# Behind the mixers of a two-layer hybrid decoder: gates and projections with the tokens stationary, two retention heads as one block group

## The chip, the cores and the metric

The kernel runs on one core of one Trainium2 chip. The metric is the device time of one execution in microseconds (us), as the median of several runs. Of the core's engines this text uses TensorE (PE for its matmuls, PEld for its weight loads), VectorE (DVE), ScalarE (ACT), GpSimd (POOL) and SyncE (SP). The last two, and ACT, also issue DMA transfers; SP's and ACT's go through hardware queues, POOL's through a software queue.

## The reference

Two layers on an input x of 512 tokens by 1024 channels, float32. This is what the change touches of a layer:

```python
z = jnp.einsum('bsd,dc->bsc', x, w_in) + b_in
q_a, k_a, v_a, q_r, k_r, v_r, g_r, gate_a, gate_b = jnp.split(z, SPLIT_POINTS, axis=-1)
...
y_a = jnp.sum(wts[..., None] * jnp.stack(outs, axis=0), axis=0)     # attention, 384 wide
y_r = _retention(...)                                               # 4 heads of 512
y_b = (jax.nn.silu(g_r) * y_r.reshape(B, S, RET_V_WIDTH)).astype(x.dtype)
merged = (jax.nn.sigmoid(gate_a) * jnp.einsum('bsc,cd->bsd', y_a, w_attn_proj)
          + jax.nn.sigmoid(gate_b) * jnp.einsum('bsc,cd->bsd', y_b, w_ret_proj))
return jnp.einsum('bsd,de->bse', merged, w_out)
...
x = _layer_norm(ALPHA * x + mix, ln1_g[l], ln1_b[l])
```

Two mixers run side by side, dilated window attention (`y_a`) and retention with four heads (`y_b`). Each is projected to 1024 channels, each projection is multiplied by the sigmoid of 1024 columns of the input projection (`gate_a`, `gate_b`), and the sum goes through `w_out`. Then come the residual, a layer norm and a dense SwiGLU block of 2816 hidden features.

## The kernel before

**Numbers in two parts.** TensorE works on float32 rounded to its `fp32r` form. Every operand is therefore split into a high part, which ACT copies, and a low part, which DVE subtracts (`hilo`, L94 to L96), and a product is three matmuls: high with high, high with low, low with high. A weight arrives by `load` in one of eight buffers `raw` of 128x1024, and `unit` makes its two parts `whi` and `wlo`, in four buffers each.

**Block groups.** A large matrix product is cut into 2x2 blocks and done with seven block products in place of eight (Strassen's scheme in Winograd's form). On the left stand A11, A12, A22 and the four sums S1 to S4 of x, held in `xh`, `xl` and `xs`; on the right B11, B12, B21, B22 and sums of them that are made from the weights. A block product adds into one of a few PSUM banks, and what remains are a few additions of 512 columns. `wide` (L426) runs such a group with the weights stationary and 256 tokens moving, `tall` (L397) with 128 tokens stationary and up to 512 weight columns moving. `biased` (L482) is `tall` with a bias row: a matmul of one row of `pick` with `bh` puts the bias into PSUM first.

**Order of the work.** The program is written in the order of TensorE's work. Smaller pieces of it (turns, normalisations, loads) stand in a list `side`; after each three matmuls `tick` takes from it at a given rate (`rate`, `pace`, `drain`). Each engine runs its instructions in its own order, and a DMA that waits holds the DMAs behind it in the same engine's order. The buffers' release sets when SP can issue a load: a `raw` buffer is free when DVE has made the low part of the weight in it.

**The stages around the change**, in each layer:

1. The sigmoid columns (`gates`, L1087). Four pieces of 256 columns of `gate_a` paired with the same of `gate_b`, by `wide`. A result has the features on the partitions, so the bias goes into ACT's sigmoid, on 128x256. The sigmoids of `gate_a` stay in `sg`; those of `gate_b` go to `g_d` in DRAM (ACT's queue).
2. The attention projection (L1126 to L1143). `w_attn_proj` is stationary, the tokens move: 8 tiles of 9 matmuls of 512. DVE multiplies each tile with its `sg`, and POOL writes the product to `g_d`. Retention's output y is read back from `y_d` around this time: its first half is split into `xs`, the rest into `xh` and `xl`, whose x is no longer needed.
3. The retention projection (L1191 to L1215). For each of four pieces of 256 channels: four units of `w_ret_proj` as stationary weights, 2 x 16 x 3 matmuls of 512 tokens; then two gated additions of 128x512, and `hilo` into `m`, which has the features on the partitions, as the next stage wants it. No block group here: 384 matmuls.
4. `w_out` (L1229, `xstat`): `m` stationary, 512 columns moving, first columns 0 to 511 for all four token tiles, then the other half tile by tile; then residual, layer norm and the turn into `xh` and `xl` for the SwiGLU block.

Of the kernel before, what the change touches and what calls it, by code (L numbers as in the profile page):

```python
# [55 lines left out]
def hybrid_kernel(ctx, tc, x, rel_bias, w_in, b_in, w_attn_proj, w_ret_proj, w_out,  # L56
# [15 lines left out]
    NR = DEPTH * (RH + 2)  # L72
# [385 lines left out]

    def bias_rows():
# [4 lines left out]
        for q in (0, BK):  # L464
            for ly in range(DEPTH):
                for b2 in range(2):
                    o, e = b2 * RV, (C_VR, C_GR)[b2]
                    pool.dma_start(r[q + ly * RH:q + (ly + 1) * RH, o:o + RV],
                                   b_in[ly, e:e + RH * RV].rearrange("(h n) -> h n", h=RH))
                    e = C_VA + 2 * b2 * VB  # L470
                    pool.dma_start(r[q + va_row(ly, 0):q + va_row(ly, 2), o:o + VB],
                                   b_in[ly, e:e + 2 * VB].rearrange("(h n) -> h n", h=2))

# [34 lines left out]
    g_d = drp.tile([2, KD * P, S], F32, name="g_d")  # L508
# [169 lines left out]
    def layer(ly, cp):  # L678
# [4 lines left out]
        def bcol(c):  # L683
            return bT[:, c // P:c // P + 1]
# [304 lines left out]
        with stage("ret") as rp:  # L989
# [79 lines left out]
            ylow = xs.rearrange("p s h k t -> p (s h k t)").rearrange("p (h k t) -> p h k t", h=2, k=KD)  # L1069
            yraw = {}  # L1070

            def y_load(q):
                yraw[q] = load(y_v[:, 2 * q:2 * q + 2], 2, S)

            def y_parts(k):
                return (ylow[:, 0, k], ylow[:, 1, k]) if k < KD else (xh[:, k - KD], xl[:, k - KD])

            def y_put(q):
                if q < 4:
                    hilo(yraw[q], ylow[:, 0, 2 * q:2 * q + 2], ylow[:, 1, 2 * q:2 * q + 2])  # L1080
                else:
                    ks = slice(2 * q - KD, 2 * q - KD + 2)
                    hilo(yraw[q], xh[:, ks], xl[:, ks])

            def gates(dp, sa, sb):

                sn = {}  # L1087

                def put(o_, v, c, ts_):
# [3 lines left out]
                def ev(i, ps):  # L1093
                    p2 = ps.rearrange("p (q t) -> p q t", q=2)
                    if i in (1, 5, 6):
                        sn[i] = work("sn").rearrange("p (q t) -> p q t", q=2)
                        act.copy(out=sn[i], in_=p2)
                    elif i == 2:
                        dve.tensor_tensor(out=sn[1], in0=p2, in1=sn[1], op=ALU.add)
                        put(sa, sn[1], C_GA, slice(0, 256))  # L1100
                    elif i == 3:
                        dve.tensor_tensor(out=sn[6], in0=p2, in1=sn[6], op=ALU.subtract)
                        put(sb, sn[6], C_GB, slice(0, 256))
                    elif i == 7:
                        dve.tensor_tensor(out=sn[5], in0=sn[5], in1=p2, op=ALU.subtract)
                        put(sb, sn[5], C_GB, slice(256, 512))
                    elif i == 4:
                        put(sa, p2, C_GA, slice(256, 512))

                wide(pair_right(w_l[:, :, C_GA:], w_l[:, :, C_GB:], dp * 256), x_left, ev)  # L1110
                act.dma_start(g_d[1, dp * 256:(dp + 1) * 256].rearrange("(e p) s -> p e s", p=P), sb)

            pace(40)
            sgs, ya = [], []
# [5 lines left out]
            for dp in range(KD // 2):  # L1120
                if dp == KD // 2 - 1:
                    drain()
                    side.extend([nothing] * 4 + [lambda t=t: ya_put(t) for t in range(NG)] + [lambda q=q: y_load(q) for q in range(2)])
                    pace(18)
                sgs.append(slot("sg", F32))
                gates(dp, sgs[dp], rp.tile([P, 2, S], F32, tag="sb", name="sb"))  # L1126
            drain()
            was = [unit(load(wa_l[:, :, :256], NG, 256))]
            for dp in range(KD // 2):
                h, l = was[dp]  # L1130
                y_put(dp)
                if dp < 2:
                    y_load(dp + 2)
                if dp + 1 < KD // 2:
                    was.append(unit(load(wa_l[:, :, (dp + 1) * 256:(dp + 2) * 256], NG, 256)))
                for e in range(2):
                    cs = slice(e * P, (e + 1) * P)
# [4 lines left out]
                    dve.tensor_tensor(out=v, in0=v, in1=ps, op=ALU.mult)  # L1142
                pool.dma_start(g_d[0, dp * 256:(dp + 1) * 256].rearrange("(e p) s -> p e s", p=P), sgs[dp])  # L1143
# [4 lines left out]
        xt = fp.tile([P, NI, D], F32, name="xtok")  # L1148
# [8 lines left out]
        def norm(i, dst=None):  # L1157
            xi = xt[:, i]
# [12 lines left out]
        def residual(i, hf, ps, first, last):  # L1171
            o_ = xt[:, i, hf * 512:(hf + 1) * 512]
# [7 lines left out]
        with stage("mp") as mp:  # L1180

            m = mp.tile([P, 2, KD, S], F32R, name="m")
            xc = [[mp.tile([P, 4, 256], F32, name=f"xc{a}{b}") for b in range(2)] for a in range(2)]
            res = x if ly == 0 else spill
            pool.dma_start(xt, res.rearrange("(i p) d -> p i d", p=P))
            ln_par(mp.tile([P, 2 * D], F32, name="lnp"), ln1_g[ly], ln1_b[ly])

            def wr_unit(dp, h):
                return unit(load(wr_l[:, 4 * h:4 * h + 4, dp * 256:(dp + 1) * 256], 4, 256))

            for dp in range(KD // 2):  # L1191
                us = [wr_unit(dp, h) for h in range(2)]
                if dp == 0:
                    for q in range(4, 8):
                        y_load(q)
                    for q in range(4, 8):
                        y_put(q)
                us += [wr_unit(dp, h) for h in range(2, RH)]
                va, vb = (load(rows(g_d[b, dp * 256:(dp + 1) * 256]), 2, S) for b in range(2))
                pss = [psum("ps") for _ in range(2)]  # L1200
                for hh, (h, l) in enumerate(us):
                    for e in range(2):
                        cs = slice(e * P, (e + 1) * P)
                        for t in range(4):
                            k = 4 * hh + t
                            yh, yl = y_parts(k)
                            mm3(pss[e], h[:, t, cs], l[:, t, cs], yh, yl, k == 0, k == 4 * RH - 1)
                            tick(STEP)
                for e in range(2):
                    d = 2 * dp + e  # L1210
                    sa, sb = va[:, e], vb[:, e]
                    dve.tensor_tensor(out=sb, in0=sb, in1=pss[e], op=ALU.mult)
# [231 lines left out]
```

## Time and profile before

| | |
|---|---|
| median of 3 runs | 2108.03 us (2107.03 to 2109.09) |
| the profiled execution | 2107.58 us, span 2105.4 us, mean granted TensorE clock 0.999 |
| PE busy | 2089.3 us, 99% of the span |
| DVE, ACT, POOL busy | 1585.6 us (75%), 1114.0 us (53%), 260.5 us (12%) |
| moved by DMA | 363.91 MB, a mean of 173 GB/s |
| one execution of the four stages in layer 0 | gates within 476 to 565.65 us, attention projection to 582.0, retention projection to 669, then `w_out` |

The profile lists the busy time of each engine, the chain of work that ended last, groups of instructions by line (count, busy time, mean duration of one, idle time in front of them and what ended it), the DMA issues, and a timeline. A matmul's listed duration is its whole passage through the pipelined array; what it costs is the distance to the next one, which the chain gives: a stretch of the chain divided by its matmuls. Within a gates stage of the first layer, 30 matmuls and 16 turns of the retention stage before it are mixed in.

### The profile page before, as it was taken

How to read it: one execution, taken by the hardware profiler on the slowest of the kernel's cores; microseconds unless marked ns; L12 is line 12 of the kernel's file. 1: busy time of each engine (PE TensorE's matmuls, PEld its weight loads, DVE VectorE, ACT ScalarE, POOL GpSimd, SP SyncE). 2: the span in 40 equal slices, each digit the busy share in tenths (PEclk: the TensorE clock that was granted, in tenths of full speed). 3: DMA queues.
4: the chain of work that ended last, by engine and by line, in shares of the span. 5: the costliest groups of instructions: out<-in, count | busy, mean ns of one | idle time of the engine just before them, and what ended most of it. 6: DMA issues, size and time to landing. Idle time of an engine off the chain costs nothing.

```text
span 2105.4 us, 34894 instructions
## 1 busy us (share of the span) xinstructions
PE 2089.3 (99%) x13818; PEld 1898.4 (90%) x13818; DVE 1585.6 (75%) x2281; ACT 1114.0 (53%) x1723; POOL 260.5 (12%) x265
## 2 busy tenths in 40 slices
PE   9999999999999999999999999999999999999998
PEld 8989888889988898999899898888899889989897
DVE  7666888787644798887787578887867357988876
ACT  5567655556623364555355765555666233655551
POOL 4111111111000101111030111111000001110101
PEclk9999999999999999999999999999999999999999
DMA  8966467677776168868258555758677761687771
GB/s 245 218 169 146 125 156 180 178 187 175 228 265 200 44 155 206 193 164 216 85 158 224 146 129 132 193 142 209 164 195 242 237 200 36 174 196 177 194 195 42
DMA packets 319940, 363.91 MB, mean 173 GB/s; under 512 B 22429, under 2 KB 251969, under 8 KB 319648
## 3 DMA queue, kind: packets, MB, share of 16 engines
q1 hardware_dynamic: 229888, 257.20, 39.5%
q0 software_dynamic: 62608, 91.68, 23.2%
q10 hardware_dynamic: 27280, 12.80, 2.1%
q8 instruction: 108, 1.77, 0.3%
q14 instruction: 56, 0.46, 0.1%
HBM read 335.84 MB, written 28.53 MB: 173 GB/s over the span
## 4 chain that ended last, share of the span: by engine, by line
PE 92%; issue 4%; DVE 1%; DMA 1%; ACT 1%; POOL 0%; SPq 0%; POOLq 0%; DVEq 0%; ACTq 0%
PE ps L84 83%; PE px L84 6%; DMA raw<-in_w_in 1%; PE px L576 1%; PE px L1035 1%; PE px L193 0%; DVE wlo L351 0%; POOL ry L135 0%; ACT whi L345 0%; PE px L642 0%; DVE xtok L1167 0%; DMA raw<-in_w_ffn_gate 0%; ACT s L566 0%; DVE raw L363 0%; DVE raw L367 0%
## 5 line engine op out<-in xcount | busy, mean ns | idle before, releaser
L345 ACT CAST whi<-raw 128x1024 fp32r<-128x1024 f32 (+1 forms) x518 | 519.9, 1008 | 466.1 <-PE ps L84 198.8
L351 DVE TENSOR_TENSOR wlo<-raw,whi 128x1024 fp32r<-128x1024 f32 (+1 forms) x518 | 604.5, 1171 | 206.9 <-ACT whi L345 193.5
L84 PE MATMUL ps<-xs,whi 128*128 128x256 f32 (+1 forms) x2944 | 571.9, 293 | 0.4 <-ACT sn L807 0.4
L84 PEld LDWEIGHTS ps<-xs,whi 128*128 128x128 f32 x2944 | 467.5, 191 | 15.0 <-issue 1.7
L84 PE MATMUL ps<-xs,wlo 128*128 128x256 f32 (+1 forms) x1472 | 430.2, 292 | 0.6 <-DVE wlo L351 0.6
L84 PE MATMUL ps<-xh,whi 128*128 128x256 f32 (+1 forms) x1424 | 422.6, 298 | 2.7 <-ACT xh L95 2.2
L84 PE MATMUL ps<-xl,whi 128*128 128x256 f32 (+1 forms) x1424 | 419.5, 295 | 0.0
L84 PE MATMUL ps<-xh,wlo 128*128 128x256 f32 (+1 forms) x1424 | 418.7, 295 | 0.0
L84 PEld LDWEIGHTS ps<-xs,wlo 128*128 128x128 f32 x1472 | 281.6, 191 | 6.1 <-DVE wlo L351 1.1
L84 PEld LDWEIGHTS ps<-xh,whi 128*128 128x128 f32 x1424 | 271.0, 191 | 15.8 <-ACT xh L95 3.5
L84 PEld LDWEIGHTS ps<-xl,whi 128*128 128x128 f32 x1424 | 272.2, 191 | 8.3 <-DVE xl L96 0.6
L84 PEld LDWEIGHTS ps<-xh,wlo 128*128 128x128 f32 x1424 | 271.8, 191 | 6.5
L84 PE MATMUL ps<-whi,xs 128*128 128x512 f32 (+1 forms) x768 | 225.0, 362 | 0.8 <-ACT sn L490 0.8
L336 POOL DMA_DIRECT2D raw<-in_w_in x80 | 98.8, 1257 | 690.6 <-DVE wlo L351 271.8
L96 DVE TENSOR_TENSOR wlo<-raw,whi 128x1024 fp32r<-128x1024 f32 (+2 forms) x78 | 88.8, 1140 | 124.6 <-ACT whi L95 124.3
L367 DVE TENSOR_TENSOR raw<-raw 128x1024 f32<-128x1024 f32 (+1 forms) x148 | 173.8, 1174 | 8.0 <-DMA raw<-in_w_in 5.8
L84 PE MATMUL ps<-whi,ht 128*128 128x512 f32 x544 | 170.1, 391 | 0.0
L84 PEld LDWEIGHTS ps<-whi,xs 128*128 128x128 f32 x768 | 137.7, 188 | 20.3 <-ACT sn L490 1.0
L95 ACT CAST whi<-raw 128x1024 fp32r<-128x1024 f32 (+2 forms) x78 | 76.5, 982 | 140.1 <-PE ps L84 92.1
L84 PE MATMUL ps<-wlo,xs 128*128 128x512 f32 (+1 forms) x384 | 138.2, 360 | 0.3 <-DVE wlo L351 0.3
L84 PEld LDWEIGHTS ps<-whi,ht 128*128 128x128 f32 x544 | 101.8, 188 | 22.3 <-DVE ht L96 1.5
L336 POOL DMA_DIRECT2D raw<-in_w_ffn_gate x40 | 51.7, 1292 | 522.3 <-DMA raw<-in_w_ffn_up 222.6
(222 smaller groups left out, 2974.5 us busy)
## 6 DMA issues: line engine op xcount, KB each, us to landing
raw<-in_w_in SPq DMA_DIRECT2D x168, 512.0 KB, 5.0
raw<-in_w_in POOLq DMA_DIRECT2D x64, 512.0 KB, 8.1
raw<-in_w_ffn_up SPq DMA_DIRECT2D x64, 512.0 KB, 4.6
raw<-in_w_ffn_down SPq DMA_DIRECT2D x52, 512.0 KB, 4.7
raw<-in_w_ffn_gate SPq DMA_DIRECT2D x44, 512.0 KB, 4.9
raw<-in_w_ffn_gate POOLq DMA_DIRECT2D x40, 512.0 KB, 7.2
raw<-in_w_ret_proj SPq DMA_DIRECT2D x32, 512.0 KB, 6.7
raw<-in_w_in SPq DMA_DIRECT2D x56, 256.0 KB, 4.8
```

Of the source, the lines that this page charges most:

```text
L84: pe.matmul(ps, lhsT=a, rhs=b, start=start, stop=stop, skip_group_check=True)
L95: act.copy(out=hi, in_=src)
L96: dve.tensor_tensor(out=lo, in0=src, in1=hi.bitcast(F32), op=ALU.subtract)
L336: pool.dma_start(r, self.src({"P1": "B12", "P3": "B22"}[n], u), accum_op=ALU.add)
L345: act.copy(out=h, in_=src)
L351: dve.tensor_tensor(out=l, in0=src, in1=h.bitcast(F32), op=ALU.subtract)
L367: dve.tensor_tensor(out=r, in0=r, in1=self.t["B22" if n == "P2" else "B21", u], op=ALU.add)
L576: pe.transpose(px[:, hh, j * P:(j + 1) * P], ss[od][:, hh, j * P:(j + 1) * P], ident)
L1035: pe.transpose(px[:, t * P:(t + 1) * P], ys[i][:, t * P:(t + 1) * P], ident)
```

## The change

- **Gates.** Two pieces of 512 columns of `gate_a` with the same of `gate_b`, by `biased` and so `tall`: tokens stationary, 512 columns moving. The results have the tokens on the partitions; the bias is a matmul of `pick` with `bh`, whose new rows are filled at the start (`gate_row`, 8 more small DMAs of POOL); the sigmoid is one ACT instruction of 512 columns.
- **Attention projection.** The tokens `ya` are stationary, 512 columns of `w_attn_proj` move. 8 tiles of 9 matmuls of 512, as before; a tile is now 128 tokens by 512 channels. `g_d` is `[2, S, D]`, tokens first.
- **Retention projection.** Heads 0 and 1 (1024 of the 2048 rows of `w_ret_proj`) are one block group of seven products, tokens stationary; heads 2 and 3 are added plainly into the same banks, 4 units for columns 0 to 511 and 4 for the rest. That makes 7 x 24 + 8 x 24 = 360 matmuls. The sums on the right are made by DMA: `p1`, one buffer for two units, is loaded with B11 by SP, and POOL adds B12, then B22, then B21 to it with accumulating DMAs; B12 + B22 is made in two `raw` buffers in the same way. The sums of y on the left are `x_sums`, on DVE and ACT. y is held in `xh`, `xl` (heads 0 and 1, and part of head 3), `xs` (the sums) and a new buffer `yp`.
- **The gated mix** comes out with tokens on the partitions, so TensorE turns it: 8 groups of four transposes of 128x128, in the `side` list, and `hilo` fills `m` from PSUM.
- **`w_out`** goes over the tokens in another order, `xtok` is two tiles, and `xc` and `lnp` come later.

The core of the diff:

```diff
-    g_d = drp.tile([2, KD * P, S], F32, name="g_d")
+    g_d = drp.tile([2, S, D], F32, name="g_d")
...
-            def gates(dp, sa, sb):
...
-                    for q in range(2):
-                        act.activation(out=o_[:, q, ts_], in_=v[:, q], func=AF.Sigmoid, bias=bcol(c + (2 * dp + q) * P))
...
-                wide(pair_right(w_l[:, :, C_GA:], w_l[:, :, C_GB:], dp * 256), x_left, ev)
+            def gates(c):
...
+                return biased(halves(w_l, 0, (2, 2), C_GA + c * S, C_GB + c * S, S), S, gate_row(ly, c), left, right)
...
+            more = [lambda: y_put(1, 1)] + x_sums(yb)
+            b11 = [load(block_w("B11", u), 2, S) for u in range(2)]
+            for hf in range(2):
+                if hf:
+                    u11 = [unit(r) for r in b11]
+                for i in range(NI):
                     ps = psum("ps")
-                    for t in range(NG):
-                        mm3(ps, h[:, t, cs], l[:, t, cs], ya[t][:, 0], ya[t][:, 1], t == 0, t == NG - 1)
-                    v = sgs[dp][:, e]
+                    ks = [(u, k) for u in was[hf] for k in range(u[0].shape[1])]
+                    for t, ((h, l), k) in enumerate(ks):
+                        yh, yl = (ya[t][:, e, i * P:(i + 1) * P] for e in range(2))
+                        mm(ps, yh, h[:, k], t == 0, False)
+                        mm(ps, yh, l[:, k], False, False)
+                        mm(ps, yl, h[:, k], False, t == NG - 1)
+                    v = sga[i][:, hf]
                     dve.tensor_tensor(out=v, in0=v, in1=ps, op=ALU.mult)
-                pool.dma_start(g_d[0, dp * 256:(dp + 1) * 256].rearrange("(e p) s -> p e s", p=P), sgs[dp])
+                    pool.dma_start(g_d[0, i * P:(i + 1) * P, hf * S:(hf + 1) * S], v)
...
+                def p_load(u, b, add):
+                    if add:
+                        pool.dma_start(p1[u], block_w(b, u), accum_op=ALU.add)
+                    else:
+                        nc.sync.dma_start(p1[u], block_w(b, u))
...
+                def gated(i, hf, v):
+                    g = gv[i, hf]
+                    dve.tensor_tensor(out=g[:, 1], in0=g[:, 1], in1=v, op=ALU.mult)
+                    dve.tensor_tensor(out=g[:, 0], in0=g[:, 0], in1=g[:, 1], op=ALU.add)
+                    turns[i] += 1
+
+                    def turn():
+                        turns[i] -= 1
+                        px = psum()
+                        for d in range(4):
+                            pe.transpose(px[:, d * P:(d + 1) * P], g[:, 0, d * P:(d + 1) * P], ident)
+                        ks, ts_ = slice(4 * hf, 4 * hf + 4), slice(i * P, (i + 1) * P)
+                        hilo(px.rearrange("p (d t) -> p d t", d=4), m[:, 0, ks, ts_], m[:, 1, ks, ts_])
+
+                    side.extend([nothing] * (i % 2 == 0) * 2 + [turn])
...
+                yq = [load(y_v[:, 8 + 2 * q:10 + 2 * q], 2, S) for q in range(4)]
+                u21 = [unit(load(block_w("B21", u), 2, S)) for u in range(2)]
+                while more:
+                    more.pop(0)()
+                for q, r in enumerate(yq[:3]):
+                    hilo(r, yp[:, 0, 2 * q:2 * q + 2], yp[:, 1, 2 * q:2 * q + 2])
+                hilo(yq[3].rearrange("p e (h t) -> p (e h) t", h=2), xh[:, 0:4, 256:S], xl[:, 0:4, 256:S])
+                for u in range(2):
+                    p_load(u, "B11", False)
+                for u in range(2):
+                    p_load(u, "B12", True)
+
+                A = pair()
+                product("A11", u11, A, True)
+                ahead = unit(load(plain_w(0, 0), 2, S))
+                sn1 = copies(A)
+                X = pair()
+                product("A12", u21, X, True)
+                Y = pair()
+                for u in range(4):
+                    now = ahead
+                    if u < 3:
+                        ahead = unit(load(plain_w(u + 1, 0), 2, S))
+                    else:
+                        for i in range(2):
+                            g_load(i, 0)
+                        ahead = p_units()
+                    plain(u, now, X + Y)
...
+                product("S2", now, A, False)
...
+                product("S3", now, A, False)
...
+                product("A22", ahead, A, False)
```

What the scheduler makes of it is not the written order. These are DVE's instructions in layer 0 at the attention projection (each `sg<-sg,ps` is the product of one tile) and the start of the retention projection. Before:

```order
L1142 TENSOR_TENSOR sg<-sg,ps 128x512
L96 TENSOR_TENSOR wlo<-raw,whi 128x768
L1142 TENSOR_TENSOR sg<-sg,ps 128x512
L96 TENSOR_TENSOR xl<-raw,xh 128x1024
L1142 TENSOR_TENSOR sg<-sg,ps 128x512
L96 TENSOR_TENSOR wlo<-raw,whi 128x1024
L96 TENSOR_TENSOR xl<-raw,xh 128x1024
L1142 TENSOR_TENSOR sg<-sg,ps 128x512
```

In the change, from the last three tiles on (`xl` here is the low part of `yq[3]`, the four `xs` of this stage are the sums S1 to S4, `yp` the low parts of `yq[0]` to `yq[2]`, and the last row's first `wlo` is that of the first plain unit):

```order
L1142 TENSOR_TENSOR sg<-sg,ps 128x512 x2
L213 TENSOR_TENSOR raw<-raw 128x1024
L1142 TENSOR_TENSOR sg<-sg,ps 128x512
L96 TENSOR_TENSOR xl<-raw,xh 128x4x256
L96 TENSOR_TENSOR xs<-raw,xs 128x1024
L1142 TENSOR_TENSOR sg<-sg,ps 128x512
L213 TENSOR_TENSOR raw<-raw 128x1024
L96 TENSOR_TENSOR wlo<-raw,whi 128x1024 x2
L96 TENSOR_TENSOR xs<-raw,xs 128x1024
L96 TENSOR_TENSOR yp<-raw,yp 128x1024 x3
L96 TENSOR_TENSOR wlo<-raw,whi 128x1024 x4
```

Between the tiles there were one or two splits before. Now the sums of y and their splits, the rest of y and the units of three products stand between and behind them.

SP's order of the loads from there on in the change (`p_6144` is `p1`, the four `y_d` are `yq`, and of the six `in_w_ret_proj` behind them the first two are B21, the others the plain units):

```order
L113 DMA raw<-y_d 128x4x256 x2
L113 DMA raw<-in_w_ret_proj 128x2x512 x2
L1208 DMA p_6144<-in_w_ret_proj 128x2x512 x2
L113 DMA raw<-y_d 128x2x512 x4
L113 DMA raw<-in_w_ret_proj 128x2x512 x6
L113 DMA raw<-g_d 128x2x512 x2
```

And POOL's, in the same place (`L1206` are the accumulating loads, the first two add B12 to `p1`):

```order
L1152 DMA xtok<-in_x 128x2x1024
L1206 DMA p_6144<-in_w_ret_proj 128x2x512
L1143 DMA g_d<-sg 128x512
L1206 DMA p_6144<-in_w_ret_proj 128x2x512
L1143 DMA g_d<-sg 128x512 x7
L1206 DMA p_6144<-in_w_ret_proj 128x2x512 x2
L1311 DMA raw<-in_w_ret_proj 128x2x512 x2
L1206 DMA p_6144<-in_w_ret_proj 128x2x512 x2
```

Before, POOL had there only `xtok` and four writes of `g_d`. The loads of `p1` stand ahead of the four `yq` on SP and wait for memory that held `sb` until its last write to `g_d`; the first accumulating load stands ahead of the first `g_d` write on POOL.

More of the change, by code (lines that the diff above doesn't have):

```diff
@@ L1122, in layer @@
+            pace(40)
+            run(gates(0))
+            for n_, _ in enumerate(gates(1)):
+                if n_ == 2:
                     drain()
-                    side.extend([nothing] * 4 + [lambda t=t: ya_put(t) for t in range(NG)] + [lambda q=q: y_load(q) for q in range(2)])
+                    side.extend([nothing] * 4 + [lambda t=t: ya_put(t) for t in range(NG)] + [lambda b=b: y_block(0, b) for b in range(2)])
                     pace(18)
-                sgs.append(slot("sg", F32))
@@ L1126, in layer, with block_w @@
-                gates(dp, sgs[dp], rp.tile([P, 2, S], F32, tag="sb", name="sb"))
             drain()
[L1128 to L1137, printed above, removed]
-                    ps = psum("ps")
-                    for t in range(NG):
-                        mm3(ps, h[:, t, cs], l[:, t, cs], ya[t][:, 0], ya[t][:, 1], t == 0, t == NG - 1)
-                    v = sgs[dp][:, e]
+            def block_w(b, u):
+                k = 4 * (b[1] == "2") + 2 * u
+                c = (b[2] == "2") * S
+                return wr_l[:, k:k + 2, c:c + S]
@@ new lines, in plain_w @@
+            def plain_w(u, hf):
+                return wr_l[:, 2 * RH + 2 * u:2 * RH + 2 * u + 2, hf * S:(hf + 1) * S]
+            was = [[unit(load(wa_l[:, o:o + n, hf * S:(hf + 1) * S], n, S)) for o, n in ((0, 2), (2, 1))] for hf in range(2)]
+            for b in range(2):
+                y_put(0, b)
+            for b in range(2):
+                y_block(1, b)
+            more = [lambda: y_put(1, 1)] + x_sums(yb)
[4 more added lines that the diff above has]
+                for i in range(NI):
+                    ps = psum("ps")
+                    ks = [(u, k) for u in was[hf] for k in range(u[0].shape[1])]
[5 more added lines that the diff above has]
+                    v = sga[i][:, hf]
@@ L1147, in layer, with xtok @@
         fp = fin.enter_context(stage("fin", side="right"))
-        xt = fp.tile([P, NI, D], F32, name="xtok")
+        xt = [fp.tile([P, 2, D], F32, name="xtok")]
+        res = (x if ly == 0 else spill).rearrange("(h i p) d -> h p i d", p=P, h=2)
+        pool.dma_start(xt[0], res[0])
+        def xtok(i):
+            return xt[i // 2][:, i % 2]
         lnp = []
@@ L1182, in layer @@
             m = mp.tile([P, 2, KD, S], F32R, name="m")
[L1183 to L1207, printed above, removed]
-                            tick(STEP)
[L1209 to L1212, printed above, removed]
-                    dve.tensor_tensor(out=sa, in0=sa, in1=sb, op=ALU.add)
-                    hilo(sa, m[:, 0, d], m[:, 1, d])
@@ new lines, in layer, with m_tok, evo @@
+            with stage("lp") as lp:
+                xc = [[lp.tile([P, 4, 256], F32, name=f"xc{a}{b}") for b in range(2)] for a in range(2)]
+                xt.append(fin.enter_context(stage("fin2", side="right")).tile([P, 2, D], F32, name="xtok"))
+                pool.dma_start(xt[1], res[1])
+                ln_par(lp.tile([P, 2 * D], F32, name="lnp"), ln1_g[ly], ln1_b[ly])
+                wo_l = rows(w_out[ly])
+                def m_tok(k, i):
+                    return m[:, 0, k, i * P:(i + 1) * P], m[:, 1, k, i * P:(i + 1) * P]
+                def evo(hf, i, ps):
@@ L1226, in evo @@
                         norm(i)
-                        side.extend([nothing] * (6, 2, 4, 5)[i] + to_xT(xt[:, i], i, xc))
-                raws = [load(wo_l[:, k:k + 2, hf * 512:(hf + 1) * 512], 2, 512) for k in range(0, KD, 2)]
-                xstat([unit(r) for r in raws] if hf == 0 else tail_units(raws), 512, m_tok, evo, token_outer=(hf == 1))
+                        side.extend([nothing] * (6, 2, 5, 4)[i] + to_xT(xtok(i), i, xc))
+                raws = [load(wo_l[:, k:k + 2, :S], 2, S) for k in range(0, KD, 2)]
+                units = [[unit(r) for r in raws]]
+                raws = [load(wo_l[:, k:k + 2, S:], 2, S) for k in range(0, KD, 2)]
+                units.append(tail_units(raws))
+                for hf, toks in ((0, (0, 1)), (1, (0,)), (1, (1,)), (0, (2, 3)), (1, (2,)), (1, (3,))):
+                    while any(turns[i] for i in toks):
+                        side.popleft()()
+                    xstat(units[hf], S, m_tok, lambda i, ps, hf=hf: evo(hf, i, ps), toks=toks)
         fo = fin.enter_context(stage("fo", 4))
```

162 lines of the change are left out of this document (115 added, 47 removed).

## The prediction

> **What bounds the kernel now.** I read the busy times first, then what TensorE waits for, then the chain in the stages that change, and last the DMA queues there.
>
> ```profile
> PE 2089.3 (99%) x13818; PEld 1898.4 (90%) x13818; DVE 1585.6 (75%) x2281; ACT 1114.0 (53%) x1723; POOL 260.5 (12%) x265
> ```
>
> TensorE is busy in 99% of the span of 2105.4 us. What it waits for while it computes is small; the view of its waits has seven rows, and the first three hold 4.6 us:
>
> ```profile
> PE ps L84 <- ACT xh L95: 2.2, 4, 1.4
> PE px L84 <- DVE warm L825: 1.5, 1, 1.5
> PE ps L84 <- DVE wlo L351: 0.9, 3, 0.4
> ```
>
> So the time is the number of matmuls times the distance between them, and it changes by what is taken off TensorE, less any new stall. The distances come from stretches of the chain of waits that hold one shape (start, length, what, count): the gates' 256 columns, a turn of four transposes, the retention projection's 512 columns with the weights stationary, and those of `w_out` with the tokens stationary.
>
> ```profile
> 499.62 17.69 PE ps L84 x147
> 517.30 0.44 PE px L1035 x4
> ...
> 581.94 55.08 PE ps L84 x243
> ...
> 667.85 38.08 PE ps L84 x168
> ```
>
> 17.69 / 147 = 0.1203 us for 256 columns; 55.08 / 243 = 38.08 / 168 = 0.2267 us for 512, whichever side is stationary; 0.44 us for a turn. Per column the wider form costs 0.443 ns and the narrow one 0.470: the 256-column matmul carries some 14 ns beyond half a wide one.
>
> **What is removed and added on TensorE, per layer.**
>
> - Gates: four pieces of 7 x 24 = 672 matmuls of 256 become two pieces of 7 x 24 = 336 of 512. 672 x 0.1203 = 80.8; 336 x 0.2267 = 76.2; -4.6 us. The same columns pass; only the 14 ns are saved.
> - The bias rows: 8 matmuls of 512 more, +1.8 us. Bias matmuls run in other stages; their passage through the array is nearly that of `w_out`'s matmuls in the groups below (396 and 389 to 393 ns), so I price them alike.
> - Attention projection: 72 matmuls of 512 both times, 16.3 us. Nothing.
> - Retention projection: 8 x 48 = 384 become 7 x 24 + 8 x 24 = 360; -24 x 0.2267 = -5.4 us. Making one half of the depth a block group saves an eighth of that half, a sixteenth of the whole.
> - Turns: 8 groups x 0.44 = +3.5 us.
>
> ```profile
> L84 PE MATMUL ps<-xs,m 128*128 128x512 f32 x192 | 45.5, 393 | 0.0
> L84 PE MATMUL ps<-whi,m 128*128 128x512 f32 x128 | 39.7, 389 | 0.0
> ...
> L84 PE MATMUL ps<-bh,pick 128*128 128x512 f32 x32 | 12.7, 396 | 0.0
> ```
>
> Sum: -4.6 + 1.8 - 5.4 + 3.5 = -4.7 us per layer; with unrounded factors -4.6. Two layers: **-9.2 us**. The profiled execution took 2107.58 us, 2.2 more than its span and 0.45 less than the median; I leave both as they are. Without any new stall: 2107.6 - 9.2 = 2098.4.
>
> What costs nothing: the eight bias DMAs at the start (TensorE's start waits for x and weights; at worst under 1 us); the sigmoids without bias (fewer, longer, on ACT, 53% busy); the writes of `g_d` by token tile (same bytes).
>
> **What the change adds off TensorE, and whether it is hidden.** The gates stage and the two projections are these windows (start:end, length, then busy and count of PE, PEld, DVE, ACT, POOL, the clock, the share of the DMA engines, GB/s):
>
> ```profile
> 476.39:565.65 89.26, 89.26 (x719) 87.99 (x718) 61.94 (x78) 58.01 (x87) 6.45 (x5) 1.00 0.67 179
> 565.65:582.00 16.35, 16.35 (x74) 13.53 (x73) 14.12 (x16) 8.71 (x10) 2.54 (x4) 1.00 1.01 364
> 582.00:670.00 88.00, 88.00 (x390) 72.87 (x389) 41.46 (x47) 26.16 (x28) 2.21 (x4) 1.00 0.68 229
> ```
>
> In the retention projection DVE was busy 41 of 88 us, and the change adds some 6 units of splits and the gated work there: hidden as a sum. The tight place is the attention projection: DVE 14.1 of 16.35 us and the DMA engines full before anything is added. Call its start T0 (565.65 here). DVE's spacing comes from its timeline:
>
> ```profile
> 579.56 1.22 DVE L96 TENSOR_TENSOR xl<-raw,xh 128x1024 fp32r<-128x1024 f32 x1
> 580.70 0.68 DVE L1142 TENSOR_TENSOR sg<-sg,ps 128x512 f32<-128x512 f32 x1
> 581.29 1.22 DVE L96 TENSOR_TENSOR xl<-raw,xh 128x1024 fp32r<-128x1024 f32 x1
> ```
>
> 1.14 us from a 1024-wide operation to the next instruction, 0.60 from a 512-wide one. In the changed order, from just before T0 to the low part of the first plain unit, DVE has 19 operations of 1024 (4 sums, 4 `xs`, 2 `xl`, 3 `yp`, 6 `wlo`) and 9 of 512: 19 x 1.14 + 9 x 0.60 = 27.1 us. TensorE needs that low part when the attention projection (16.3), A11 (24 x 0.2267 = 5.4) and A12 (5.4) are done: T0 + 27.2. **There is no slack: what DVE idles before that, TensorE stalls.** In the first tiles DVE idles about 0.3 us for a tile, which the start just before T0 makes up to within 0 to 0.7 us.
>
> DVE's order has one operand that comes late: `yq[3]`, the last of the four y loads. DVE reaches its low part at T0 + 15.0 (behind the seventh tile, 7 x 2.04 + 0.6), so the load must land by 14.0 for ACT's cast of 1 us. SP can issue it only when DVE frees the buffer of the first B11 unit, worked through DVE's order at T0 + 11. That leaves 3 us. How long does such a load take?
>
> ```profile
> raw<-y_d SPq DMA_DIRECT2D x16, 512.0 KB, 5.0
> raw<-in_w_ret_proj SPq DMA_DIRECT2D x32, 512.0 KB, 6.7
> raw<-in_w_in POOLq DMA_DIRECT2D x64, 512.0 KB, 8.1
> ```
>
> 5.0 us in the median; and in the change POOL's two accumulating loads of `p1` and its `g_d` writes fall into the same time: `p1` is loaded at T0 + 0 to 2, lands some 4 us later, the two accumulating loads start about T0 + 7. Such loads are costly. Two windows with accumulating loads of `w_in` in flight, and with plain traffic:
>
> ```profile
> 418.00:421.00 3.00, 3.00 (x26) 2.92 (x25) 2.32 (x4) 0.82 (x1) 0.74 (x1) 1.00 1.10 200
> ...
> 576.00:583.00 7.00, 7.00 (x33) 5.79 (x32) 5.98 (x8) 2.84 (x3) 1.45 (x2) 1.00 1.03 407
> ```
>
> Full engines move 200 GB/s with them and 407 without: 512 KB of an accumulating load fill all engines for about 2.8 us, of a plain one for 1.4. How SP's hardware queue fares beside POOL's software queue is told by the load that SP issued last before the retention projection, the second of this pair (issued by 570.6), against the 2 MB `xtok` that POOL issued after it, and by ACT's wait for it:
>
> ```profile
> 568.77 1.84 SPq L113 DMA_DIRECT2D raw<-in_w_ret_proj  x2
> ...
> 572.06 0.77 POOL L1185 DMA_DIRECT2D xtok<-in_x  x1 [47.19 <-DVE xl L96]
> ...
> 584.48 1.05 ACT L95 CAST whi<-raw 128x1024 fp32r<-128x1024 f32 x1 [5.50 <-DMA raw<-in_w_ret_proj]
> ```
>
> It took 14 us. The queue table of the DMA view for 577.84 to 584.38 us (packets, MB, share), and below it the same for 421 to 423 us, beside accumulating loads:
>
> ```profile
> q0 software_dynamic: 689, 2.65, 100.4%
> q1 hardware_dynamic: 49, 0.05, 2.0%
> ...
> q0 software_dynamic: 139, 0.27, 74.2%
> q1 hardware_dynamic: 113, 0.23, 34.2%
> ```
>
> So the hardware queue gets between almost nothing and about a third of the engines while the software queue has work. With a third from T0 + 7 on, `yq[2]` (issued at 9.3) lands about 14, `yq[3]` about 16.4; with nothing until both accumulating loads (5.7 us) and the four or five `g_d` writes between them (0.7 each) are through, `yq[3]` lands about 18.3. DVE idles 2.4 to 4.3 us, plus the 0 to 0.7: a stall of 2.4 to 5.0 us per layer. Neither end excludes the other in the rows; I take 3.6. The same work returns in layer 1: **+7.2 us**.
>
> [...]
>
> After this place, margins are small but there. `p1`'s next sums have some 25 us each. The four turns that TensorE meets late come from gated additions that I place 0.6 to 1.3 us before they are needed, and when TensorE has stalled earlier, DMA and DVE are further ahead of it. I take 0; losing each once would be 1 to 2 us per layer.
>
> **Sum:** 2107.6 - 9.2 + 7.2 = **2105.6 us**; own range 2103 to 2109 (2.4 to 5.0 us per layer: 2103.2 to 2108.4, and a little for the turns).
>
> **The rivals.**
>
> - *The loads land in time* (faster). If POOL's accumulating loads are over before `yq[2]` and `yq[3]` are issued, or these land in 3 to 3.5 us, 0 to 0.7 us per layer remain: 2098.4 to 2099.8, say 2099.5; with half of the stall, 2102. For it: `w_attn_proj`'s loads of 384 KB, in a quieter time, took 3.0 us in the median (row below), and the accumulating loads could start early if `p1` lands early. Against: the engines were full in this window before (share 1.01).
> - *The first load of `p1` is late* (slower). It waits for the last write of `sb` to `g_d`, and the four `yq` stand behind it in SP's order. Such a write took 3.8 us in the median (row below), and here it meets full engines. If it takes 6, then `p1` lands about T0 + 9, the accumulating loads fill T0 + 11 to 17 with the `g_d` writes, just where `yq[3]` and B21's two units are due, and a hardware queue that gets nothing brings `yq[3]` at T0 + 22 or later and the plain unit behind it likewise: about 9.4 us per layer, 2107.6 - 9.2 + 18.8 = 2117. It is slower than before from 4.6 us per layer, measurably from 6.7.
>
> ```profile
> g_d<-sb ACTq DMA_DIRECT2D x8, 512.0 KB, 3.8
> raw<-in_w_attn_proj SPq DMA_DIRECT2D x8, 384.0 KB, 3.0
> ```
>
> - *The change does not do what it says on TensorE*: tokens stationary might not run at 0.2267 us. If the gates ran at the narrow form's price per column, 4.6 us per layer more would make any case 9 us longer: 2115 with the forecast's stall. `w_out` above, at 0.2267 us with the tokens stationary, speaks against it. I give it 0.03, inside the slower case.
>
> **How the numbers follow.** The stall with a contended queue, 2105.6: 0.50. Loads in time: 0.33. `p1` late: 0.17, with the small ones in it. A change under 0.2%, 4.2 us, cannot be told from none here. The first case lies mostly within (under 2103.8 is faster: stalls below about 2.6 us per layer): 0.06 faster, 0.42 same, 0.02 slower. The second: 0.30 faster, 0.03 same. The third: 0.02 same, 0.15 slower. Together faster 0.36, same 0.47, slower 0.17. The range must take in the case in time and part of the late one: 2098.5 to 2111.5.
>
> **What would show it.** PE's count of 256-column matmuls down by 1344 and its sum of busy time by about 9; a row of TensorE's waits on the low part of the first plain unit (`wlo`, DVE L96) of 2.4 to 5 us twice, with ACT waiting for `yq[3]`'s DMA before it: that is the forecast. No such row and a span near 2096 to 2098: the first rival. The wait at 9 us, with SP's first `p1` load issued after T0 + 3: the second. A chain of the new gates with more than 0.235 us per matmul: the third. Waits of TensorE on the `px` turns, or of the turns on gated additions, would say that I placed the margins behind wrongly, and a stall anywhere in the gates stage that the whole walk starts wrongly.

## The result, and the profile after

The change made the kernel slower. The median of 4 runs is 2130.1 us (2127.6 to 2131.8) against 2108.6 us before; the ratio is 1.0099, with a 95% interval of 1.0081 to 1.0116. The forecast was 2105.6, no change. The profiled execution took 2127.56 us with a span of 2125.8 us, 20.4 more than before.

The busy times on the page after:

```profile
PE 2091.5 (98%) x13178; PEld 1867.7 (88%) x13178; DVE 1623.9 (76%) x2327; ACT 1129.2 (53%) x1725; POOL 285.6 (13%) x299
```

TensorE has 640 instructions fewer, as the counts said, and yet is busy 2 us longer: part of them ran slowly (granted clock 0.50 to 0.51 in three stretches). Its waits after, where before the first row had 2.2 us:

```profile
PE ps L84 <- ACT whi L95: 9.7, 2, 5.0
PE ps L84 <- ACT sn L496: 5.7, 3, 3.3
PE ps L84 <- DVE wlo L351: 2.6, 3, 1.4
PE ps L84 <- DVE wlo L96: 2.0, 3, 0.9
```

To see where the time went I took from each trace the start of the first matmul of each stage. The table has each stage's length less that of before, in us. "Start" is up to the first attention scores; "projections" go from the attention projection's first matmul to the first of `w_out`, and `w_out` up to its last. The last column but one is what lies between: no edit touches those stages, and their sum varies by up to 4 us from one profile to the next, so single entries of the table carry more than the spans.

| kernel | start | gates 0 | projections 0 | `w_out` 0 | gates 1 | projections 1 | `w_out` 1 | rest | span |
|---|---|---|---|---|---|---|---|---|---|
| the change | +4.1 | -0.7 | +6.8 | +2.2 | +1.4 | +6.4 | +1.9 | -1.7 | +20.4 |
| e1: no first accumulating loads | +2.9 | +1.7 | +0.4 | +2.3 | +4.5 | +0.8 | +3.3 | -2.4 | +13.5 |
| e2: `p1` late | +4.4 | -0.9 | +0.3 | +2.2 | +2.3 | +0.3 | +2.1 | -2.2 | +8.5 |
| e3: bias rows on SP | +1.8 | -0.4 | +6.9 | +2.2 | +3.3 | +6.8 | +3.3 | -3.3 | +20.7 |
| e4: y casts behind the copy | +3.8 | -2.4 | +6.0 | +2.3 | -2.5 | +5.4 | +2.0 | -3.5 | +11.1 |
| e8: late quarters of y | +4.3 | -0.5 | -1.3 | +2.4 | +3.4 | -2.7 | +2.1 | -3.6 | +4.0 |
| e5: e2, e3, e4 | +1.2 | -2.4 | -0.6 | +2.1 | -1.0 | +0.2 | +2.2 | +0.2 | +2.0 |
| e6: e2, e3, e4, e8 | +0.9 | -2.4 | -2.7 | +2.2 | -2.1 | -2.7 | +3.3 | -3.5 | -7.0 |
| e7: no block group | +1.6 | -2.4 | +3.1 | +1.5 | -1.5 | +3.1 | +1.6 | -1.8 | +5.2 |

By TensorE's count the gates should have given -2.8 per layer, and the projections with `w_out` -1.9: six of the eight turns fall before `w_out`, so -2.8 and +0.9. `w_out` shows 1.0 to 1.3 us more than that in the change, but what follows layer 1's `w_out` is 0.6 to 0.9 us shorter in every row, so part of it only moved. Three places lost time: the start, the gates, and above all the projections. Some scatter has a known cause: the gates of e1 in both layers, those of layer 1 in e2, e3 and e8, and the rest of e5 each hold 3.4 us in which TensorE was granted half its clock (0.50 in e1's layer 0, 0.51 in e2), which is 1.7 us of its work; the last section comes back to this.

**Behind the attention projection** (T0 = 569.0 in layer 0). First SP's queue, then ACT, DVE, in the timelines of the changed kernel:

```profile
572.26 0.88 SPq L1208 DMA_DIRECT2D p<-in_w_ret_proj  x2
573.19 7.39 SPq L113 DMA_DIRECT2D raw<-y_d  x4
581.36 18.36 SPq L113 DMA_DIRECT2D raw<-in_w_ret_proj  x6
...
589.78 1.05 ACT L95 CAST xh<-raw 128x1024 fp32r<-128x1024 f32 x1 [11.07 <-DMA raw<-y_d]
594.55 1.04 ACT L95 CAST whi<-raw 128x1024 fp32r<-128x1024 f32 x1 [2.77 <-DMA raw<-in_w_ret_proj]
597.01 1.04 ACT L95 CAST whi<-raw 128x1024 fp32r<-128x1024 f32 x1 [1.42 <-DMA raw<-in_w_ret_proj]
...
590.86 1.23 DVE L96 TENSOR_TENSOR xl<-raw,xh 128x1024 fp32r<-128x1024 f32 x1 [6.60 <-ACT xh L95]
```

The first load of `p1` went out at T0 + 3.2. `yq[3]` was issued at 580.2, T0 + 11.2, as forecast, and landed at T0 + 20.7 after 9.5 us; ACT stood 11 us before its cast, DVE 6.6 us before its low part. B21's two units behind it landed at T0 + 25.4 and 27.9, for a product that was due at T0 + 21.8. The queue table of 580 to 583 us shows what SP's loads met, and that of 586 to 589 below it:

```profile
q0 software_dynamic: 271, 0.62, 93.8%
q1 hardware_dynamic: 71, 0.14, 12.4%
...
q0 software_dynamic: 224, 0.62, 66.9%
q1 hardware_dynamic: 218, 0.44, 40.2%
```

The engines were full from about T0 + 7 to 27, and in these two rows the hardware queue had an eighth and two fifths of them. TensorE waited 4.7 us, and then did not come back at once (start:end, length, busy and count of PE, PEld, DVE, ACT, POOL, granted clock, DMA share, GB/s):

```profile
590.50:595.60 5.10, 0.45 (x2) 0.03 (x1) 4.09 (x4) 2.32 (x3) 0.54 (x1) 1.00 1.03 404
595.60:602.40 6.80, 6.25 (x14) 4.52 (x15) 4.67 (x4) 5.39 (x7) 0.00 (x0) 0.51 0.81 262
602.40:607.00 4.60, 4.00 (x17) 2.97 (x17) 4.60 (x5) 4.20 (x5) 0.00 (x0) 0.98 0.82 258
```

After the pause the granted clock was 0.51 for 6.8 us; a matmul of 512 columns took 427 ns in place of 227, and TensorE was 2.4 us slower over this stretch. Little of that counts in the end, because the low part of the first plain unit came late anyway, by DMA, ACT and DVE, and TensorE still waited for it:

```profile
606.10 0.50 PE L84 MATMUL ps<-wlo,yp 128*128 128x512 f32 x1 [0.60 <-DVE wlo L96]
```

**In the gates**, ACT in layer 1 and TensorE's matmul that waited for it:

```profile
1601.81 1.04 ACT L95 CAST xh<-raw 128x1024 fp32r<-128x1024 f32 x1 [4.40 <-DMA raw<-y_d]
1602.76 1.04 ACT L345 CAST whi<-raw 128x1024 fp32r<-128x1024 f32 x1
1603.71 0.58 ACT L496 COPY sn<-ps 128x512 f32<-128x512 f32 x1
...
1604.34 0.50 PE L84 MATMUL ps<-whi,xs 128*128 128x512 f32 x1 [3.25 <-ACT sn L496]
```

The cast of the first y block stands in ACT's order ahead of the copy that frees a PSUM bank, and its load was late; the same in layer 0, for 1.3 us.

**At the start**, POOL in the kernel before, and after:

```profile
23.62 0.55 POOL L529 DMA_DIRECT2D bias_r<-bias_d  x1 [3.53 <-DMA bias_d<-bv]
```

```profile
29.01 0.55 POOL L535 DMA_DIRECT2D bias_r<-bias_d  x1
43.55 0.55 POOL L939 DMA_DIRECT2D bias<-bias_r  x1 [13.99 <-DMA bias_r<-bias_d]
```

This 2.7 MB transfer went out 5.4 us later: the eight new DMAs for the bias rows stand ahead of it, and now also the loads of `cos` and `sin`, which wait for TensorE. SP's weight loads beside it landed together with it or behind it, at 44 to 45 us in place of 40 to 41, and TensorE waited 2.2 us for low parts (0.2 before). Another 1.6 of the 4.1 us are not of this kind. From 18.9 to 22.3 us TensorE had half its clock, in this one of the ten profiles, and why is open:

```profile
18.80:22.30 3.50, 3.50 (x19) 3.50 (x18) 1.67 (x3) 1.75 (x4) 2.79 (x6) 0.51 0.70 220
```

### The profile page after: what moved, and what is told of

The parts are those of the page before. It is cut to its first block, busy times and chain, and to the rows that moved or that the text cites. A ratio compares the mean times of both kernels' runs of the same rounds, so it can differ in the third digit from the quotient of the medians.

```text
span 2125.8 us, 33803 instructions
## 1 busy us (share of the span) xinstructions
PE 2091.5 (98%) x13178; PEld 1867.7 (88%) x13178; DVE 1623.9 (76%) x2327; ACT 1129.2 (53%) x1725; POOL 285.6 (13%) x299
## 5 line engine op out<-in xcount | busy, mean ns | idle before, releaser
L84 PE MATMUL ps<-xs,whi 128*128 128x256 f32 x2176 | 399.5, 284 | 0.4 <-ACT sn L813 0.4
L84 PE MATMUL ps<-whi,xs 128*128 128x512 f32 (+1 forms) x1152 | 348.2, 372 | 5.7 <-ACT sn L496 5.7
L84 PEld LDWEIGHTS ps<-xs,whi 128*128 128x128 f32 x2176 | 339.4, 192 | 4.9 <-issue 1.7
L84 PE MATMUL ps<-xh,whi 128*128 128x256 f32 (+1 forms) x1104 | 318.4, 290 | 2.2 <-ACT xh L95 1.9
L84 PE MATMUL ps<-xl,whi 128*128 128x256 f32 (+1 forms) x1104 | 315.5, 286 | 0.0
L84 PE MATMUL ps<-xh,wlo 128*128 128x256 f32 (+1 forms) x1104 | 315.1, 286 | 0.0
L84 PE MATMUL ps<-xs,wlo 128*128 128x256 f32 x1088 | 308.0, 283 | 2.6 <-DVE wlo L351 2.6
L84 PEld LDWEIGHTS ps<-xh,whi 128*128 128x128 f32 x1104 | 210.4, 191 | 10.2 <-ACT xh L95 3.4
L84 PE MATMUL ps<-whi,xh 128*128 128x512 f32 (+1 forms) x464 | 177.2, 382 | 9.7 <-ACT whi L95 9.7
L84 PE MATMUL ps<-wlo,xh 128*128 128x512 f32 (+1 forms) x464 | 174.3, 376 | 1.4 <-DVE wlo L96 1.4
L84 PE MATMUL ps<-whi,xl 128*128 128x512 f32 (+1 forms) x464 | 173.8, 375 | 0.0
```

The source lines that it names most:

```text
L84: pe.matmul(ps, lhsT=a, rhs=b, start=start, stop=stop, skip_group_check=True)
```

## The experiments

**e1, e2: which transfers hold `yq[3]`?** e1 leaves out the first two accumulating loads; e2 keeps all and moves `p1`'s loads and those two behind what is urgent.

```diff
 e1
-                for u in range(2):
-                    p_load(u, "B12", True)
 e2
+                with tc.issue_after(lastld[0].ins), tc.issue_after(wrote.ins):
-                for u in range(2):
-                    p_load(u, "B11", False)
-                for u in range(2):
-                    p_load(u, "B12", True)
+                    for u in range(2):
+                        p_load(u, "B11", False)
+                    for u in range(2):
+                        p_load(u, "B12", True)
```

(`lastld` is the last load of B21 on SP, `wrote` the last `g_d` write on POOL; the lines only order the queues.)

> The first two accumulating loads of each layer (B12 onto p1) are left out, so the product S1 uses B11 in place of B11 + B12; nothing else moves. Theory, full DMA engines: in the changed kernel yq[3] was issued at T0 + 11.2 and landed at T0 + 20.7, because it shared the engines with these two loads (some 2.8 us of all engines each) and the g_d writes. Without them it lands about 5.6 us earlier, T0 + 15, and the stall of TensorE behind the attention projection goes from 9.4 us per layer to 1 to 4: 2113 to 2120 us, from 2130. Rival, the order on SP: yq[0] and yq[1] stood behind p1's late first load (issued T0 + 3.2), and everything moved by that; nothing of it changes here: 2128 to 2131.

> The loads of p1 with B11 go behind the two units of B21 on SP, and the first two accumulating loads behind the last g_d write on POOL; all else keeps its order. Theory, full DMA engines: 1 MB of plain loads (2.8 us of all engines) and 1 MB of accumulating ones (5.6 us) leave the time before yq[3], which then lands 3.5 to 5 us after its issue, T0 + 14.5 to 16; a stall of 0.7 to 2 us per layer is left of 9.4, and no stretch at half clock: 2112 to 2116. Rival, late buffers: yq[3] and the B21 units wait for raw buffers in any case, and 5 us or more stay per layer: 2121 or more.

e1 took 2118.2 us (2117.8 to 2120.7), e2 2116.7 us (2115.3 to 2117.5; ratio to before 1.0036, 1.0023 to 1.0049). The projections lost 5.7 to 6.5 us less per layer in both, and there was no half clock behind them (mean granted clock 0.997 in e1 and 0.998 in e2, against 0.995 in the change). Beside 0.3 to 0.4 us at a turn, of the waits between 560 and 700 us this is left in e1, and below it in e2:

```profile
PE ps L84 <- DVE wlo L96: 2.5, 2, 1.4
...
PE ps L84 <- DVE wlo L96: 2.4, 2, 1.6
```

In e1 `p1`'s first load was as late as in the change (T0 + 2.7) and the four `yq` still stood behind it, so a late `p1` and its place in SP's order do not make the loss by themselves: the accumulating loads are needed for it. `yq[3]`, issued at T0 + 11 in both, landed at T0 + 16.9 in e1 and 17.3 in e2, against 20.7; the `g_d` writes show the same (DMA view of the change, then of e1):

```profile
g_d<-sg POOLq DMA_DIRECT2D x16, 256.0 KB, 11.5
```

```profile
g_d<-sg POOLq DMA_DIRECT2D x16, 256.0 KB, 5.8
```

e2 fell just short of what was expected of it: `yq[3]` still took 5.8 us, not 3.5 to 5, and layer 1's gates had a stretch at half clock.

**e8: the same accumulating loads, but nothing late at the head of the queues.**

```diff
-                yq = [load(y_v[:, 8 + 2 * q:10 + 2 * q], 2, S) for q in range(4)]
+                def y_late(q):
+                    t = load(y_v[:, 8 + 2 * q:10 + 2 * q], 2, S)
+                    ...    # the same split as before
...
+                y_late(0)
...
                         ahead = unit(load(plain_w(u + 1, 0), 2, S))
+                        y_late(u + 1)
```

> Of retention's heads 2 and 3, only the first quarter of y is loaded and split before the first plain unit; each other quarter comes one unit ahead of its use. The loads of p1 and the accumulating loads stay where the change has them. Theory, a late operand at the head of DVE's and ACT's queue: the engines stood still for yq[3], which TensorE needs only in the fourth plain unit, 28 us later. B21's units now take yq's place on SP, are issued 6 to 8 us earlier and land by T0 + 12; the stall of 9.4 us per layer goes to 0 to 1 though the DMA engines are as full: 2110 to 2115, from 2130. Rival, the accumulating loads alone decide: whatever stands behind them lands late, and 4 us or more per layer stay: 2119 or more.

2112.5 us (2110.6 to 2119.3). The projections now gain 1.3 and 2.7 us, with the accumulating loads in place. B21's units were issued at T0 + 4.0 and landed at T0 + 10.2 and 11.5. The DMA engines were as full (581 to 586 us, the change, then e8; the last two columns are their share and GB/s), and the `g_d` writes took 10.9 us in the median:

```profile
581.00:586.00 5.00, 5.00 (x23) 4.14 (x23) 3.26 (x5) 0.00 (x0) 2.01 (x4) 1.00 1.09 283
```

```profile
581.00:586.00 5.00, 5.00 (x24) 4.14 (x23) 4.57 (x6) 1.80 (x2) 2.04 (x4) 1.00 1.07 276
```

But the late loads of 10 to 13 us moved to where nearly all of them were covered (0.9 us of TensorE's waiting was left in layer 0). Between T0 + 10 and 22, where DVE had stood still for 6.6 us, its largest gap was 0.43 us:

```profile
583.85 0.69 DVE L1142 TENSOR_TENSOR sg<-sg,ps 128x512 f32<-128x512 f32 x1
584.96 1.23 DVE L96 TENSOR_TENSOR xs<-raw,xs 128x1024 fp32r<-128x1024 f32 x1 [0.43 <-ACT xs L95]
```

So the accumulating loads and an order that puts an operand needed 28 us later ahead of one needed at once were both necessary; taking away either removes most of the stall. Full engines alone do not make it: in e1, from 581 to 584 us, they were as full, but moved 412 GB/s in place of 253 to 283. e8 changes SP's order and that of ACT and DVE together; how much each gives was not separated.

**e4: the gates.** The copy of S1's second half is named, and the first two y casts go behind it.

```diff
-                act.copy(out=sn[i, a], in_=ps)
+                cp_ = act.copy(out=sn[i, a], in_=ps)
+                if i == 5:
+                    sn5_copy[0] = cp_
...
-            for b in range(2):
-                y_put(0, b)
+            with tc.issue_after(sn5_copy[0].ins):
+                for b in range(2):
+                    y_put(0, b)
```

> In the gates' second half the casts of the first two blocks of y are put behind the second copy of product S1 on ACT. Theory: ACT stood 3.9 us (layer 0) and 4.4 us (layer 1) before such a cast, waiting for the block's load, with a weight cast and the copy that frees a PSUM bank queued behind it, and TensorE waited 1.5 and 3.4 us for the copy. Behind it, both waits go: 4 to 5 us less, 2125 to 2126. Rival: the sums of y, which need these casts, come later and the stall only moves behind the attention projection: 2129 to 2131.

2121.3 us (2118.3 to 2123.6), some 4 us better than expected. The gates give -2.4 and -2.5 us, nearly the -2.8 of the count, and TensorE has no wait in that stage. That is 5.6 us of the gain; the rest lies in stages with no edit and is not explained.

**e3: the start.**

```diff
-                    pool.dma_start(r[q + gate_row(ly, 0):q + gate_row(ly, 2), o:o + S],
+                    nc.sync.dma_start(r[q + gate_row(ly, 0):q + gate_row(ly, 2), o:o + S],
```

> The eight new small DMAs that fill the gates' bias rows are issued by SP, not POOL. Theory: on POOL they put the 2.7 MB load bias_r 5.4 us later (29.0 in place of 23.6 us), and SP's weight loads behind it landed at 44 to 45 in place of 40 to 41 us; TensorE lost 4.06 us up to the first attention scores. With the rows on SP bias_r is back at about 24 us and 3 to 4 us come back: 2126 to 2127, from 2130. Rival: the loss comes from the larger bias operand (its cast and subtraction stand in ACT's and DVE's order) and stays: 2129 to 2131.

2129.2 us (2125.0 to 2131.7): by the time alone not told apart from 2130.1. In its profile `bias_r` went out at 25.9 us, TensorE's wait for low parts there was 0.6 us in place of 2.2, and the start lost 1.8 us in place of 4.1:

```profile
25.92 0.55 POOL L535 DMA_DIRECT2D bias_r<-bias_d  x1 [5.10 <-DMA bias_d<-bv]
```

All the traces together say more than this one time. From TensorE's turn of `sin` (at 25.8 us in the kernel before) to its first `ps<-whi,xh` (at 55.5), the five profiles with the rows on POOL are 1.5 to 2.8 us longer than before, and the four with the rows on SP 0.3 to 0.6. So about 2 us of the start's loss came from the rows on POOL's queue. In e3's time it does not show, at least partly because layer 1's gates lost 1.9 us more in its profile than in the change, with a stretch at half clock that the change does not have there.

**e5, e6: together.** e5 has the edits of e2, e3 and e4; e6 that of e8 as well.

> The three edits of before together: p1's loads late, the gates' bias rows on SP, the first y casts behind the copy. If the three places are independent, their steps in the profiles add: 13 us behind the attention projection, 5.5 in the gates, 2.3 at the start, from a span of 2125.8 to 2105, a time of 2106 to 2109, equal to the kernel before. Rival, a shared resource: what one edit frees another place takes up, and 2112 or more is measured.

> All four edits: the three of before and the late quarters of y. What is left is the sum on TensorE: 9.2 us per execution less than before, and of the stalls the 0.4 us per layer at the turns and 1 to 2 us at the start: 2099 to 2103, faster than the kernel before by 0.2 to 0.4%. Rival, the margins that the prediction called small (turns, p1's next sums) now open: 2104 to 2108.

e5: 2107.1 us (10 runs, 2104.0 to 2109.1), ratio to before 0.9994 (0.9984 to 1.0003): the same. e6: 2101.3 us (2100.1 to 2102.8), ratio 0.9968 (0.9955 to 0.9980): faster than before, and than the change by 29 us. All of e6's waits:

```profile
PE px L1255 <- issue: 1.8, 2, 1.5
PE px L84 <- DVE warm L837: 1.5, 1, 1.5
PE ps L84 <- ACT xh L95: 1.4, 4, 0.7
PE ps L84 <- DVE wlo L353: 0.9, 3, 0.4
PE px L195 <- DVE xtok L1182: 0.7, 1, 0.7
PE ps L84 <- ACT sn L819: 0.3, 1, 0.3
```

No wait for an operand of the two projections is left; the first row is two waits at the last turns, inside `w_out` (0.3 and 1.5 us by layer).

**e7: the block group undone**, with the rest as in e6: heads 0 and 1 are plain units too, `product`, `p_load` and the sums are gone.

```diff
-                A = pair()
-                product("A11", u11, A, True)
-                ...
+                for n, (u, hf) in enumerate(queue):
+                    if u == 0:
+                        pss = [psum("ps") for _ in range(NI)]
+                    fetch(n + 2)
+                    ...
+                    plain(u, units_.pop((u, hf)), pss)
```

> Undo one part of the change alone: the block group over heads 0 and 1. All four heads of the retention projection are 8 plain units for each half of the columns, 384 matmuls per layer; no sums of y or weights, no accumulating loads, quarters of y ahead of their use; tokens stationary, the turns, and the two edits at the start and in the gates stay as in the version with four edits (2101.3 us). Theory, TensorE's count decides once loads are in time: 24 matmuls more are 5.4 us per layer, and the last four gated tiles end together, with 2 us per layer before the next stage: 2112 to 2117. Rival, the group's sums and accumulating loads cost about what its 24 matmuls save: 2100 to 2106.

2112.2 us (2109.8 to 2117.1), ratio to before 1.0020 (1.0010 to 1.0029). The projections took 5.8 us more per layer than in e6, against 5.4 for 24 matmuls; the 2 us at the end of the stage did not appear (`w_out` took less than in e6). With its loads in time the block group is worth what its matmuls are, and without it the rest of the change, turns included, does not pay.

## Why the prediction was wrong, by its steps

- **The counts and prices on TensorE held.** In e6 the gates give -2.4 and -2.1 us (forecast -2.8), the projections -2.7 each (by count -2.8 with the six turns that fall there), and TensorE is busy for 2082.5 us, 6.8 less than before. The span is 7.0 us shorter than before where the sum said 9.2: the start took 0.9, the gates 1.1 against their count and `w_out` 3.7 against its own, 1.8 of it in the turns' waits, while the stages that no edit touches gave 3.5, which is not explained. Small slips of the sum do not matter beside this: with unrounded factors it is -4.8 per layer, not -4.6; a 256-column matmul carries 7 ns beyond half a wide one, and 14 only in a pair; 512 KB at 200 and 407 GB/s take 2.6 and 1.3 us, not 2.8 and 1.4.
- **The stall behind the attention projection was at the right place and too small.** The step "I take 3.6" failed: the change lost 9.6 and 9.2 us there against its count, two thirds of which e1 and e2 bring back. The rule that the step used held. "What DVE idles before that, TensorE stalls": between T0 and the low part of the first plain unit DVE idled 9.4 us in layer 0 and 9.1 in layer 1, and in e1 3.3 and 3.6, where the projections lost 3.2 and 3.6. What I had wrong is how long DVE idles. `yq[3]` landed at T0 + 20.7 and 22.2, not 16.4 to 18.3, and DVE stood still for 6.6 and 8.2 us. And I counted one late load only: B21's units behind it took 13 us each, and in layer 0 DVE waited another 1.9 us for them. So TensorE's wait was first for B21's high part, one product ahead of the low part that I had named.
- **Why `yq[3]` was so late.** The accumulating loads began at T0 + 7.6, near the 7 of the likely case, but the second landed only at T0 + 19.7, and the `g_d` writes took 11.5 us in the median. At 2.8 us for each accumulating load and 0.7 for a write, even the forecast's worst end had the software queue through by T0 + 16.
- **The second rival came by its size, with half of its reason.** It priced 9.4 us per layer at a chance of 0.17, and its sign came: `p1`'s first load went out at T0 + 3.2, behind the last write of `sb`. But it let that late load push the accumulating loads to T0 + 11, and they began at 7.6. e1 has `p1` as late and loses little. What it had right is that the hardware queue had little, 12 to 41% of the engines from 580 to 589 us, while they were in flight and `yq[3]` and B21 were due. Whether an earlier `p1` load would have cured it was not tried.
- **The half clock** was in no step. Behind this stall (granted clock 0.51 and 0.50) it made TensorE 2.4 us slower in layer 0 and 2.0 in layer 1, but nearly all of that fell into time in which TensorE would have waited: for the first plain unit's low part it still waited 0.6 us in layer 0, and in layer 1 it came 0.2 us after it was ready. At the start it cost 1.6 us.
- **The gates.** "A stall anywhere in the gates stage" stood among the signs of a wrong walk, with no price. I had followed DVE's order from T0 on, and ACT's not at all: the y cast ahead of the copy in ACT's order was there to read. It cost 1.7 and 3.8 us, the difference that e4 makes.
- **"The eight bias DMAs at the start ... at worst under 1 us"** failed: the start lost 4.1 us, 1.6 of it at half clock, and about 2 come back with them on another queue. They are small, but behind them in POOL's order stood a transfer of 2.7 MB, and behind that in time SP's weights.
- **The share of the hardware queue.** I took it between almost nothing and a third of the engines. In this place it had 12% (71 packets against 271, 580 to 583 us) and later 40% (218 against 224, 586 to 589 us). But even the larger share would hardly have been enough. At 0.44 MB in 3 us, as in the second of the two, the 3 MB of `yq` and B21 take some 21 us, an estimate, and the first of them was issued only 17.6 us before TensorE was due to use the last.

From 2107.6 - 9.2, the second rival's 18.8, the start's 4.1 and the gates' 2.1 and 4.2 against their count make 2127.6, where the profiled execution took 2127.56; that the parts agree so well is partly luck: `w_out` (2.3 us over its count in both layers) and the untouched stages (1.7 us shorter) are left out and nearly cancel.

## What to carry to other kernels

Where a queue is in order, ask of every operand at its head when it is *needed*, not only when it arrives: e8 gained 18 us by loading late what was needed late, and left the traffic as it was. Where a stage has no slack, sum the work of all queues over the stretch (here 3 MB of plain loads, 1 MB of accumulating loads at half rate (in the kernel before, 200 GB/s against 407), and 1.8 MB of writes within 20 us) before pricing any single load by its median. And read the order of every engine through the place, with what stands behind a small new DMA, before calling an edit free.

## What was not expected of the hardware

In some places a pause of TensorE had a second price. Granted clock in windows of e2: a pause of 3.3 us (from one matmul's start to the next) in layer 1, the time just after, the slow stretch, and the recovery; below them a pause of 1.5 us in layer 0 and the time after it:

```profile
1593.57:1596.83 3.26, 0.39 (x3) 0.01 (x1) 1.46 (x2) 2.53 (x4) 0.00 (x0) 1.00 0.40 128
1596.90:1597.80 0.90, 0.90 (x4) 0.77 (x5) 0.87 (x2) 0.90 (x2) 0.00 (x0) 1.00 0.00 0
1597.80:1601.20 3.40, 3.40 (x9) 2.64 (x9) 3.40 (x4) 1.92 (x2) 0.00 (x0) 0.51 0.32 55
1601.30:1605.00 3.70, 3.70 (x18) 3.06 (x17) 3.54 (x4) 1.64 (x2) 0.00 (x0) 1.00 0.50 162
...
548.40:549.88 1.48, 0.40 (x3) 0.01 (x1) 1.46 (x2) 1.48 (x3) 0.00 (x0) 1.00 0.00 0
549.90:556.00 6.10, 6.10 (x27) 5.01 (x28) 6.07 (x6) 4.14 (x5) 0.00 (x0) 1.00 0.25 86
```

After 3.3 us of pause TensorE ran at full clock for 0.9 us and then at half for 3.4 (granted clock 0.51). After 1.5 us nothing followed, and in the changed kernel (first two lines) nothing followed a pause of 3.7 us in layer 1's gates either, while in e1 (last two) a pause of 2.6 us was followed by half clock (0.50):

```profile
1600.69:1604.34 3.65, 0.40 (x3) 0.01 (x1) 1.45 (x2) 2.53 (x4) 0.00 (x0) 1.00 0.54 175
1604.34:1608.00 3.66, 3.66 (x16) 3.04 (x17) 3.63 (x4) 3.35 (x4) 0.00 (x0) 1.00 0.17 11
...
547.01:549.59 2.58, 0.39 (x2) 0.00 (x0) 1.45 (x2) 2.52 (x4) 0.00 (x0) 1.00 0.06 22
550.50:553.50 3.00, 3.00 (x8) 2.30 (x7) 2.97 (x4) 1.98 (x2) 0.00 (x0) 0.50 0.18 59
```

So no length of the pause alone decides. Nor does the time without a matmul in it: the 2.9 us of e2 and the 2.2 of e1 were followed by half clock, the 3.3 of the change were not. In the change's profile TensorE was at half clock from 18.86, 595.71 and 1650.43 us on, for 3.4, 6.8 and 6.8 us; it had been without a matmul for 4.7 us ahead of the second and for 5.0 ahead of the third. What else decides is not shown by these runs.
